# Attention scores on one core: the first k load as two transfers of 8 KB runs

## The chip, the cores and the metric

One core of one Trainium2 chip. The metric is the time of one execution on the device, in microseconds (us). In the profile, PE is TensorE's matmul, PEld its weight load, DVE is VectorE, ACT is ScalarE, POOL is GpSimd and SP is SyncE, which issues all 24 loads and outputs here (SPq in the page's table of DMA issues). "SPq" is SyncE's queue.

## The reference

```python
def setup_inputs():
    batch, heads, seq, dim = 8, 8, 512, 64
    # q and k: np.random.randn(batch, heads, seq, dim), float32

def reference(q, k):
    scale = 1.0 / np.sqrt(q.shape[-1])
    return (np.einsum('bhqd,bhkd->bhqk', q, k) * scale).astype(np.float32)
```

The inputs are 16.8 MB and the output is 67.1 MB, with little arithmetic between them.

## The kernel before

The batch is worked in four units of two. For each unit, one 2 MB transfer brings k and one brings q; GpSimd casts both to bf16 in two halves each (`s`); TensorE transposes them, VectorE and ScalarE copy the transposed tiles; matmuls make scores, and VectorE and ScalarE scale them into 4 MB output tiles. Loads and output tiles share one pool of three buffers (`big`), so the fourth unit's loads and the outputs wait until an earlier load has been cast: in the trace SyncE waits 4.9 us for GpSimd before it issues the fourth unit's k at 18.33 us, and the first evacuation, at 28.13, has waited 3.42 us for GpSimd.

```python
big_pool = ctx.enter_context(tc.tile_pool(name="big", bufs=3))
# ... (cut)
def load_and_cast(v):
    xf = big_pool.tile([P, 2, 2, J * D], f32, name="big")       # 128 x (k, q) x (s) x 2048
    both = []
    for x, src in enumerate((k_r, q_r)):
        nc.sync.dma_start(out=xf[:, x], in_=src[v].rearrange("p (s c) -> p s c", s=2))
    for x in range(2):
        xb = bf_pool.tile([P, JP, 2, D, 2], bf16, name="xb")
        wide = (1, RO)[x]
        for s in range(2):
            pinned(nc.gpsimd.tensor_copy(out=xb[:, :, s]..., in_=xf[:, x, s]...))   # (cut)
        both.append(...)
    return both
# ... (cut: transpose, rearrange)
def scores(v, t):
    o = big_pool.tile([P, 2, RO, S], f32, name="big")
    # ... 16 matmuls and 8 evacuations into o (cut)
    nc.sync.dma_start(out=out_r[v, t], in_=o.rearrange("p x i k -> p x (i k)"))
# ... (cut)
cast = [load_and_cast(v) for v in range(UNITS)]      # all loads are issued first
```

Of the kernel before, what the change touches and what calls it, by code (L numbers as in the profile page):

```python
# [1 line left out]

# [5 lines left out]


@with_exitstack  # L10
def kernel(
    ctx: ExitStack,
    tc: tile.TileContext,
    q: bass.AP,
    k: bass.AP,
    out: bass.AP,
):







    nc = tc.nc
    B, H, S, D = q.shape
    scale = 1.0 / (D ** 0.5)
    P = 128
    UNITS = B // 2
    N = H  # L30
    M = P // (2 * H)
    R = S // M
    J = R // 2
    RO = 8
    U = S // RO
    JP = J // 2
    JJ = J // RO // 2
    W = 8
    IW = W // JJ
    TILES = N // 2  # L40

    f32 = mybir.dt.float32
    bf16 = mybir.dt.bfloat16

    q_r = q.rearrange("(v b) g (m j) d -> v (b g m) (j d)", b=2, j=R)
    k_r = k.rearrange("(v b) g (m j) d -> v (b g m) (j d)", b=2, j=R)
    out_r = out.rearrange("(v b) (t x h) (u i) k -> v (b t) (h u) x (i k)", b=2, x=2, h=2, i=RO)

    consts = ctx.enter_context(tc.tile_pool(name="consts", bufs=1))

    big_pool = ctx.enter_context(tc.tile_pool(name="big", bufs=3))
    bf_pool = ctx.enter_context(tc.tile_pool(name="bf", bufs=6))
    t_pool = ctx.enter_context(tc.tile_pool(name="t", bufs=2))
    tpsum_pool = ctx.enter_context(tc.tile_pool(name="tpsum", bufs=2, space=bass.MemoryType.PSUM))
    psum_pool = ctx.enter_context(tc.tile_pool(name="psum", bufs=2, space=bass.MemoryType.PSUM))


    pinned = tc.keep_in_program_order

    n_evac = 0  # L60
    n_tp = 0

    def evacuate(dst, src):
        nonlocal n_evac
        if n_evac % 2 == 0:
            pinned(nc.scalar.mul(out=dst, in_=src, mul=scale))  # L66
        else:
            pinned(nc.vector.tensor_scalar(out=dst, in0=src, scalar1=scale, scalar2=None,  # L68
                                           op0=mybir.AluOpType.mult))
        n_evac += 1  # L70

    def half(h):
        return slice(h * D, (h + 1) * D)

    def words(ap):
        return ap.bitcast(f32)

    def load_and_cast(v):

        xf = big_pool.tile([P, 2, 2, J * D], f32, name="big")  # L80
        both = []
        for x, src in enumerate((k_r, q_r)):
            nc.sync.dma_start(out=xf[:, x], in_=src[v].rearrange("p (s c) -> p s c", s=2))
        for x in range(2):
            xb = bf_pool.tile([P, JP, 2, D, 2], bf16, name="xb")

            wide = (1, RO)[x]
            for s in range(2):
                pinned(nc.gpsimd.tensor_copy(  # L89
                    out=xb[:, :, s].rearrange("p (g i) d e -> p g e i d", i=wide),  # L90
                    in_=xf[:, x, s].rearrange("p (g e i d) -> p g e i d", e=2, i=wide, d=D)))
            both.append(words(xb.rearrange("p j s d e -> p j (s d e)")))
        return both

    def rearrange(tp, pattern, dst):

        nonlocal n_tp
        copy = (nc.vector.tensor_copy, nc.scalar.copy)[n_tp % 2]
        n_tp += 1
        for s in range(2):  # L100
            src = tp[half(s)].rearrange(pattern, n=N, h=2)
            for h in range(2):
                pinned(copy(out=dst(s, h), in_=src[:, h]))  # L103
                yield

    def transpose(v, kb, qb):


        kT = t_pool.tile([P, N, M, 2, J], bf16, name="kT")
        qz = qzs[v % 2]  # L110
        ts[v] = (kT, qz)
        kw = words(kT)
        qw = words(qz)
        for j0 in range(0, JP, W):
            tp = tpsum_pool.tile([P, W, P], f32, name="tp")
            for j in range(W):
                pinned(nc.tensor.transpose(out=tp[:, j, :], identity=identity, in_=kb[:, j0 + j]))  # L117
            yield
            yield from rearrange(tp, "d j (n h m) -> d h n m j",
                                 lambda s, h: kw[half(h), :, :, s, j0:j0 + W])  # L120
        for i0 in range(0, RO, IW):
            tp = tpsum_pool.tile([P, IW, JJ, P], f32, name="tp")
            for i in range(IW):
                for jj in range(JJ):
                    pinned(nc.tensor.transpose(out=tp[:, i, jj, :], identity=identity,  # L125
                                               in_=qb[:, RO * jj + i0 + i]))
            yield
            yield from rearrange(tp, "d i jj (n h m) -> d h i n m jj",
                                 lambda s, h: qw[half(h), i0:i0 + IW, :, h * U // 2:(h + 1) * U // 2]
                                 .rearrange("d i n (m s jj) -> d s i n m jj", s=2, jj=JJ)[:, s])  # L130

    def scores(v, t):

        kT, qz = ts[v]
        o = big_pool.tile([P, 2, RO, S], f32, name="big")
        for x in range(2):
            n = 2 * t + x
            for i in range(0, RO, 2):
                ps = psum_pool.tile([P, 2, S], f32, name="ps")
                for w in range(2):  # L140
                    pinned(nc.tensor.matmul(out=ps[:, w, :], lhsT=qz[:, i + w, n, :],  # L141
                                            rhs=kT[:, n].rearrange("d m s j -> d (m s j)"),
                                            start=True, stop=True))
                evacuate(o[:, x, i:i + 2, :], ps)
                yield
        nc.sync.dma_start(out=out_r[v, t], in_=o.rearrange("p x i k -> p x (i k)"))  # L146

    def take(steps, count):
        for _ in range(count):
            next(steps, None)  # L150

    identity = consts.tile([P, P], dtype=f32)
    make_identity(nc, identity)
    qzs = [consts.tile([P, RO, N, P], bf16, name=f"qz{n}") for n in range(2)]
    for qz in qzs:
        nc.vector.memset(qz, 0.0)  # L156
    cast = [load_and_cast(v) for v in range(UNITS)]

    ts = {}
    for _ in transpose(0, *cast[0]):  # L160
        pass
    for v in range(UNITS):
        ahead = transpose(v + 1, *cast[v + 1]) if v + 1 < UNITS else iter(())
        for t in range(TILES):
            for n, _ in enumerate(scores(v, t)):

                take(ahead, 1 if v == 0 else int(n in (0, 2, 3, 5, 6)))
        for _ in ahead:
            pass


# [1 line left out]
_INS = ['q', 'k']  # L173
_OUTS = [((8, 8, 512, 512), 'float32')]


# [23 lines left out]
```

## Time and profile before

| | before |
|---|---|
| median of 6 runs | 202.47 us (202.37 to 202.51) |
| span in the profile | 200.7 us |
| hardware DMA queue | 83.89 MB, 5504 packets, 98.3% of 16 engines' span |
| busiest engine | VectorE, 53% of the span |

Read it as a bandwidth-bound kernel: the DMA engines work nearly all of the span (98.3%) and no other engine does much over half of it (VectorE 53%).

### The profile page before, as it was taken

What the parts mean: (1) busy time and instruction counts of PE and PEld (TensorE: products, weight loads), DVE (VectorE), ACT (ScalarE), POOL (GpSimd) and SP (SyncE); (2) the same over time, 40 slices, a digit from 0 to 9 for tenths busy, and PEclk for the clock granted to TensorE, in tenths of its full rate; (3) what the DMA queues carried; (4) which work ended last, traced back from release to release, by engine and by line L of the source; (5) the groups of instructions that cost most, each with busy time, mean ns of one, the idle gap of its engine ahead of it and who ended that gap; (6) DMA issues with size and microseconds to landing.
All of it is one profiled execution on the core that took longest, in us unless ns stands there. A gap on an engine that the chain in (4) does not pass through costs nothing.

```text
span 200.7 us, 1143 instructions
## 1 busy us (share of the span) xinstructions
PE 105.3 (52%) x384; PEld 45.8 (23%) x384; DVE 106.8 (53%) x98; ACT 85.0 (42%) x97; POOL 39.5 (20%) x22
## 2 busy tenths in 40 slices
PE   0035758566657465478637496748585667510000
PEld 0034535223214131224313122312121111100000
DVE  6705538486475976485749357844444444630000
ACT  2004423864755629253844384366435243620000
POOL 1299999995000000000000000000000000000000
PEclk9999576999699999957999759975858858975555
DMA  6999999999999999999999999999999999999994
GB/s 206 424 444 437 421 421 441 434 395 421 434 424 441 428 431 431 433 426 434 431 428 424 434 441 424 431 431 434 424 431 434 431 424 431 428 437 428 428 428 199
DMA packets 5509, 83.95 MB, mean 418 GB/s; under 512 B 384, under 2 KB 384, under 8 KB 384
## 3 DMA queue, kind: packets, MB, share of 16 engines
q1 hardware_dynamic: 5504, 83.89, 98.3%
q8 instruction: 3, 0.05, 0.1%
q14 instruction: 2, 0.02, 0.0%
HBM read 16.78 MB, written 67.11 MB: 418 GB/s over the span
## 4 chain that ended last, share of the span: by engine, by line
DMA 40%; DVE 10%; PE 8%; ACT 6%; issue 1%; ACTq 0%; SPq 0%; DVEq 0%
DMA out_dram<-big 40%; DVE big L68 9%; PE ps L141 8%; ACT big L66 5%; ACT qz L103 1%; DVE qz L103 1%; ACTq L66 0%; SPq L146 0%; DVEq L68 0%
## 5 line engine op out<-in xcount | busy, mean ns | idle before, releaser
L141 PE MATMUL ps<-kT,qz 128*128 128x512 bf16 x256 | 87.6, 447 | 55.5 <-ACT big L66 41.6
L68 DVE TENSOR_SCALAR big<-ps 128x1024 f32<-128x1024 f32 x64 | 78.4, 1224 | 59.8 <-PE ps L141 37.2
L66 ACT ACTIVATE big<-ps 128x1024 f32<-128x1024 f32 x64 | 65.5, 1023 | 73.0 <-PE ps L141 37.2
L141 PEld LDWEIGHTS <-qz 128*128 128x128 bf16 x256 | 27.2, 106 | 111.0 <-issue 97.5
L89 POOL CAST xb<-big 128x2048 bf16<-128x2048 f32 x16 | 38.8, 2468 | 7.9 <-DMA big<-in_k_dram 7.3
L117 PE MATMUL tp<-identity,xb 128*128 128x128 f32 x64 | 11.6, 346 | 13.4 <-POOL xb L89 13.4
L103 ACT COPY kT<-tp 64x512 f32<-64x512 f32 x16 | 9.2, 577 | 15.3 <-PE tp L117 15.1
L103 DVE COPY kT<-tp 64x512 f32<-64x512 f32 x16 | 11.0, 686 | 6.3 <-PE tp L117 6.0
L117 PEld LDWEIGHTS tp<-identity,xb 128*128 128x128 f32 x64 | 10.5, 184 | 15.2 <-POOL xb L89 13.4
L103 DVE COPY qz<-tp 64x512 f32<-64x512 f32 x16 | 11.0, 687 | 2.7 <-PE tp L125 2.5
L103 ACT COPY qz<-tp 64x512 f32<-64x512 f32 x16 | 9.6, 602 | 2.9 <-PE tp L125 2.7
L125 PE MATMUL tp<-identity,xb 128*128 128x128 f32 x64 | 9.4, 300 | 2.5 <-ACT kT L103 2.5
L125 PEld LDWEIGHTS tp<-identity,xb 128*128 128x128 f32 x64 | 8.5, 156 | 4.3 <-issue 3.3
L156 DVE MEMSET qz<- 128x4096 uint32 x2 | 6.9, 3472 | 2.5 <-PEq L184 1.7
L103 ACT ACT_TABLE_LOAD x1 | 1.3, 1283 | 0.7 <-PEq L184 0.7
masks.py:199 POOL TENSOR_SCALAR_AFFINE_SELECT identity<-identity 128x128 f32<-128x128 f32 x1 | 0.3, 292 | 0.1
masks.py:197 POOL MEMSET identity<- 128x128 f32 x1 | 0.2, 204 | 0.3 <-POOLq L184 0.3
L184 POOL MEMSET const-float32-0.0<- 128x1 f32 x1 | 0.1, 98 | 0.2 <-issue 0.2
L184 POOL MEMSET const-bfloat16-1.0<- 128x1 bf16 x1 | 0.1, 101 | 0.0
L184 POOL MEMSET const-uint8-127<- 128x1 uint8 x1 | 0.1, 101 | 0.0
L184 POOL MEMSET const-float32-1.0<- 128x1 f32 x1 | 0.1, 98 | 0.0
## 6 DMA issues: line engine op xcount, KB each, us to landing
out_dram<-big SPq DMA_DIRECT2D x16, 4096.0 KB, 20.7
big<-in_k_dram SPq DMA_DIRECT2D x4, 2048.0 KB, 18.1
big<-in_q_dram SPq DMA_DIRECT2D x4, 2048.0 KB, 22.7
```

Of the source, the lines that this page charges most:

```text
L66: pinned(nc.scalar.mul(out=dst, in_=src, mul=scale))
L68: pinned(nc.vector.tensor_scalar(out=dst, in0=src, scalar1=scale, scalar2=None, op0=mybir.AluOpType.mult))
L89: pinned(nc.gpsimd.tensor_copy(out=xb[:, :, s].rearrange("p (g i) d e -> p g e i d", i=wide), in_=xf[:, x, s].rearrange("p (g e i d) -> p ...
L103: pinned(copy(out=dst(s, h), in_=src[:, h]))
L117: pinned(nc.tensor.transpose(out=tp[:, j, :], identity=identity, in_=kb[:, j0 + j]))
L125: pinned(nc.tensor.transpose(out=tp[:, i, jj, :], identity=identity, in_=qb[:, RO * jj + i0 + i]))
L141: pinned(nc.tensor.matmul(out=ps[:, w, :], lhsT=qz[:, i + w, n, :], rhs=kT[:, n].rearrange("d m s j -> d (m s j)"), start=True, stop=True))
L156: nc.vector.memset(qz, 0.0)
L184: nc = _bacc.Bacc("TRN2", target_bir_lowering=False, num_devices=1)
```

## The change

The intent: the first k load is 2 MB in runs of 16 KB, and GpSimd casts none of it until all has landed (at 8.53 us; the first cast starts at 8.58). Sent as two transfers, one for each half `s` of every row (8 KB runs), the first half is meant to be cast while the second is under way.

```diff
         for x, src in enumerate((k_r, q_r)):
-            nc.sync.dma_start(out=xf[:, x], in_=src[v].rearrange("p (s c) -> p s c", s=2))
+            halves = src[v].rearrange("p (s c) -> p s c", s=2)
+
+            for s in (slice(0, 1), slice(1, 2)) if v == x == 0 else (slice(0, 2),):
+                nc.sync.dma_start(out=xf[:, x, s], in_=halves[:, s])
```

## The prediction

> **What bounds the kernel now.** I read the page first: the table of busy times, the 40 slices, the DMA queues and the chain that ended last.
>
> ```profile
> span 200.7 us, 1143 instructions
> PE 105.3 (52%) x384; PEld 45.8 (23%) x384; DVE 106.8 (53%) x98; ACT 85.0 (42%) x97; POOL 39.5 (20%) x22
> ...
> DMA  6999999999999999999999999999999999999994
> GB/s 206 424 444 437 421 421 441 434 395 421 434 424 441 428 431 431 433 426 434 431 428 424 434 441 424 431 431 434 424 431 434 431 424 431 428 437 428 428 428 199
> ...
> q1 hardware_dynamic: 5504, 83.89, 98.3%
> ...
> DMA 40%; DVE 10%; PE 8%; ACT 6%; issue 1%; ACTq 0%; SPq 0%; DVEq 0%
> ```
>
> No engine is busy for more than 53% of the span, while the one hardware DMA queue fills 98.3% of the 16 DMA engines' span. The slices say where: only the first (206 GB/s) and the last (199) are half empty; the 38 between lie at 395 to 444 GB/s. The chain follows output transfers for 40% of the span and hops onto evacuations between them. That alone would look like a mixed bound, so I asked whether the DMA engines ever run out of queued work. The view of the DMA issues, cut so that each answer holds one issue, gives the time to landing; the timeline gives the start of the issue; the sum is the landing:
>
> - first k: 0.74 + 7.8 = 8.5 us. First q: 1.18 + 12.2 = 13.4. Second k: 1.66 + 16.6 = 18.3. Last q: 18.70 + 24.3 = 43.0.
> - first output: 36.81 + 17.1 = 53.9. Last output: 178.09 + 21.8 = 199.9.
>
> From the first k to the last q that is seven 2.10 MB loads in 34.5 us, 4.93 us each (425 GB/s); from the first output to the last it is fifteen 4.19 MB outputs in 146.0 us, 9.73 us each (431 GB/s). The first output is issued 6.2 us before the last load has landed, and the times to landing of the outputs (16.0 us at the least in those I read, 20.7 in the median) are all well over the 9.7 us that one output takes: when an output is issued, there are still some 6 us or more of older work in the queue. So the queue never runs dry, and computing can be late by about 6 us before the end notices.
>
> The start is the only place where the DMA engines wait for something:
>
> ```profile
> 0.74 0.39 SPq L83 DMA_DIRECT2D big<-in_k_dram  x1
> 1.18 0.42 SPq L83 DMA_DIRECT2D big<-in_q_dram  x1
> ...
> 8.58 34.34 POOL L89 CAST xb<-big 128x2048 bf16<-128x2048 f32 x14 [7.28 <-DMA big<-in_k_dram]
> ...
> 13.44 3.68 PE L117 MATMUL tp<-identity,xb 128*128 128x128 f32 x16 [13.44 <-POOL xb L89]
> ...
> 19.61 2.57 PE L125 MATMUL tp<-identity,xb 128*128 128x128 f32 x16 [2.49 <-ACT kT L103]
> ...
> 28.13 1.02 ACT L66 ACTIVATE big<-ps 128x1024 f32<-128x1024 f32 x1 [3.42 <-POOL xb L89]
> ...
> 36.81 20.11 SPq L146 DMA_DIRECT2D out_dram<-big  x3
> ```
>
> The reader is to see the relay of the opening: GpSimd waits 7.28 us for the whole first k, then casts fourteen tiles without a gap; the k transposes wait for two casts; the q transposes wait for ScalarE to empty the transposed k; the first evacuation waits for GpSimd to have done with the buffer that it will fill; the first output goes out at 36.81.
>
> [...] From the page of the profile, 98.3% of 16 x 200.7 us over the 5120 packets of data (5504 less 24 transfers x 16 small ones) is 617 ns for a 16 KB packet at the most[...].
>
> **The change part by part.** It touches one transfer of 24. The build shows one more DMA issue on the SyncE queue (two of 128 x 2048 elements for one of 128 x 4096) and a second DMA wait on GpSimd, before the second cast; the order on all engines stays.
>
> Removed: the first cast's wait for the second half of k. Half the transfer is half of 4.88 us (first k landing to first q landing), so the first half should land 2.45 us earlier, at about 6.1 us, and the first cast starts at 6.1 to 6.2 in place of 8.58.
>
> Added on SyncE: one issue, some 0.43 us. The other loads are issued that much later, q0 at about 1.6. They stand in a queue that is full until 8.5, so none of it shows.
>
> Added on the DMA engines: 128 data packets of 16 KB become 256 of 8 KB[...]
>
> Moved: the opening relay. GpSimd takes 34.34 / 14 = 2.45 us for a cast, 4.91 for the two of a load, and a load lands each 4.9 us: the two have the same pace, and GpSimd runs just one load behind. The first cast runs 6.1 to 8.6, the second half has then landed, the second runs 8.6 to 11.1. Then GpSimd needs q0, which lands at 13.4 to 13.5 as before. It waits 2.4 us there and stands where it stood. The head start is handed back at the third cast: 7.3 us of waiting becomes 4.8 + 2.4. From there on GpSimd does what it did, to 0.1 us.
>
> The k transposes do gain: 13.44 becomes about 11.1, and ScalarE ends its copies of k at about 17.2, not 19.5. The q transposes then wait for the q casts (13.5 + 4.9 = 18.4) in place of ScalarE, and start at 18.5, not 19.61: 1.1 us of the 2.4 is left. The first scores move from 23.57 to about 22.5. The first evacuation, however, waits for the eighth cast (8.58 + 8 x 2.45 = 28.2), which has not moved, so it stays at 28.1 to 28.2 and the 1.1 us end there. The first output may be issued some tenths earlier; it lies behind loads until 43.0 in any case.
>
> [...]
>
> **The rivals.**
> 1. *The head start reaches the end.* If the chain from the first cast set the end, 2.4 us would come off: 200.0 us, still within 2%. For it: the chain view names evacuations and matmuls in its early part, and GpSimd's first wait is real. Against it: the queue of loads is full until 43.0 and the outputs are queued 6 us ahead[...]. I give this 3%.
> 2. *The start-up itself changes.* First k lands at 8.5 although its bytes need 4.9: the windows view shows no packet until 1.5 us and 328 GB/s from 1.5 to 2.0, then 98 to 229 until 3.5; with half empty stretches like these the first slice is at 206 GB/s, and nearly 2 us of ramp are lost. If that ramp is paid per packet[...], 8 KB packets move half as much in it, and 0.3 to 0.9 us are lost for good: 202.8 to 203.4. If it is paid per engine once, nothing changes. [...] The profile doesn't decide between these; I take +0.3 or more to have a chance of 12%.
> 3. *The reads of 8 KB at a stride of 16 KB are slower in HBM.* Only 2.10 MB of 83.9 are read so. At half the rate that would be 4.9 us: 207 us, the only way that I see to over 2%. Nothing in the trace speaks for it; 1%.
> 4. *A new wait.* [...] an output is issued while at most two or three are in flight, so it should cost nothing.
>
> **Range and chances.** The runs of before lie within 0.1 us. Down to 202.2 for a quicker start-up or a tenth of drift, up to 202.9 for a part of rival 2 and some drift between chips. Within 2% means 198.4 to 206.5; only rival 3 leaves it upward, and I see nothing that leaves it downward, since the bytes alone need 83.89 MB / 431 GB/s = 194.6 us and the start-up, the turn from loads to outputs (10.9 us for the first output against 9.7) and the tail make up the rest: same 0.98, slower 0.01, faster 0.01.
>
> **What the changed profile would show.** Right: first cast at 6.1 to 6.2; a wait of about 2.4 us of GpSimd on q from some 11.1 to 13.5; k transposes at about 11.1; q transposes at 18.5, released by GpSimd and no longer by ScalarE; the first evacuation still at 28.1 to 28.3; 5504 + 144 = 5648 packets in the hardware queue, 400 of them small; the last load landing at 43.0 to 43.2, and a span of 200.6 to 201.0. Wrong: a last load that lands over 0.3 us later or earlier (rival 2 or 3), GpSimd without the wait at q0 (then q0 lands earlier than I think, and the first evacuation moves), or outputs that land closer to their issue than 10 us (then the queue does run dry, and the head start could matter).

The forecast's sum came to 202.5 us: 202.44 for the kernel before, 0 from the relay and less than 0.1 for the packets. That the outputs lie behind the loads in the queue is seen in the trace of before: its 24 transfers land in the order of their issue, the eight loads from 8.53 to 43.02 us and the sixteen outputs from 53.87 to 199.92.

## The result, and the profile after

The changed kernel takes 203.16 us (median of 6, 202.95 to 203.54) where the one before takes 202.47 us: ratio 1.0037, 95% interval 1.0024 to 1.0050. Ratios here and below are the mean time of one kernel's fast runs over that of the other's of the same rounds, so not quite the ratio of the medians quoted. That is within 2%, as forecast, but 0.7 us slower where less than 0.1 was forecast, and above the range's end of 202.9.

The lines of the page after that answer to those shown of before:

```profile
span 201.7 us, 1145 instructions
...
DMA  6999999999999999999999999999999999999993
GB/s 214 445 422 432 439 426 422 422 370 432 432 429 422 435 439 422 434 430 429 429 432 435 419 435 439 422 435 432 429 432 432 429 429 429 435 426 435 435 422 136
DMA packets 5653, 83.95 MB, mean 416 GB/s; under 512 B 400, under 2 KB 400, under 8 KB 400
...
q1 hardware_dynamic: 5648, 83.89, 98.0%
```

The counts are as foreseen: 144 packets more, 16 of them small. The first slice is no slower (214 against 206 GB/s). Two places differ: the ninth slice (370, before 395), and the last one (136, before 199).

The opening, from the timeline after (start, duration, instruction; in brackets the idle time before it and what ended it):

```profile
6.12 4.92 POOL L92 CAST xb<-big 128x2048 bf16<-128x2048 f32 x2 [4.82 <-DMA big<-in_k_dram]
...
11.10 3.67 PE L120 MATMUL tp<-identity,xb 128*128 128x128 f32 x16 [11.10 <-POOL xb L92]
...
13.49 29.43 POOL L92 CAST xb<-big 128x2048 bf16<-128x2048 f32 x12 [2.44 <-DMA big<-in_q_dram]
...
18.38 3.25 PE L128 MATMUL tp<-identity,xb 128*128 128x128 f32 x16 [3.60 <-POOL xb L92]
...
28.15 1.03 ACT L66 ACTIVATE big<-ps 128x1024 f32<-128x1024 f32 x1 [3.98 <-POOL xb L92]
...
43.92 4.86 POOL L92 CAST xb<-big 128x2048 bf16<-128x2048 f32 x2 [1.00 <-DMA big<-in_q_dram]
```

The first cast starts 2.46 us earlier, and GpSimd then waits 2.44 us for q: the head start is given back at the third cast. The first evacuation has not moved (28.15, before 28.13). So far all is as predicted. The last line is the one that is not: the last two casts wait 1.00 us for the last q. The line of before that answers to it:

```profile
43.17 4.86 POOL L89 CAST xb<-big 128x2048 bf16<-128x2048 f32 x2 [0.26 <-DMA big<-in_q_dram]
```

The last q lands 0.75 us later than before, though all loads ahead of it land on time. To see where, I asked for the stretch before that landing, 39.5 to 42.5 us, of both kernels (last three columns: granted clock, DMA share, GB/s by the start of packets). Before:

```profile
39.50:42.50 3.00, 2.28 (x15) 1.35 (x14) 1.53 (x2) 2.29 (x4) 3.00 (x2) 1.00 0.93 350
```

After:

```profile
39.50:42.50 3.00, 3.00 (x12) 2.08 (x11) 0.12 (x1) 1.70 (x3) 3.00 (x2) 0.50 0.96 300
```

Both fall well below the 429 GB/s of the stream around them (25 to 36 and 44 to 60 us, in both), the changed kernel further. This is the last load, with the first output standing behind it in the queue: the turn from loads to outputs. I call it the dip. The share of the engines stays near 1 (0.93 and 0.96) while the rate falls, so the engines are not idle; their packets take longer. The trace's packets show it: one of 16 KB that starts between 37 and 44 us takes 647 ns on average before and 690 after, where 614 is the average in the stream (25 to 36 us).

The landings, from the issue times and times to landing in the trace:

| us | before | after |
|---|---|---|
| first k whole | 8.53 | 8.54 |
| last k | 37.90 | 37.91 |
| last q | 43.02 | 43.77 |
| first output | 53.87 | 54.04 |
| last output | 199.92 | 200.82 |
| last k to last q | 5.13 | 5.86 |
| first to last output | 146.05 | 146.78 |

A load takes 4.9 us elsewhere (from the first k to the last, 4.88 to 4.91 each in before). So the dip costs 0.2 us before and almost 1.0 after at the last q; of the difference between the two kernels 0.17 us is left at the first output. The rest of the 0.9 us of this profiled run comes during the outputs: of the fifteen spacings between their landings eight are over 9.75 us, before four. This was the slowest run of six, and the split between the two places isn't the same in every run.

The trace keeps sixteen completions for each transfer (384 for the 24 of before), and the landing is the last of them. I read each as that of one of the sixteen engines, though the trace doesn't name it; their mean, called the average engine here, can then be followed as well:

| mean of the sixteen, us | last k | last q | first output | last output | last engine after the mean, last output |
|---|---|---|---|---|---|
| before | 37.45 | 42.60 | 52.44 | 198.68 | 1.23 |
| after | 37.31 | 42.92 | 52.75 | 198.93 | 1.89 |

For the average engine the last k comes 0.14 us sooner than before and the last q 0.32 later, and it stays 0.25 to 0.32 behind from there to the end: its outputs take no longer (146.2 us in both). So this part of the loss is made at the turn, and it is common to the sixteen: put in order, each completion of the last q comes 0.16 to 0.75 us later than its like of before. The rest, 0.66 us, is the lateness of the last completion alone, which falls further behind during the outputs: 1.28 us after the mean at the first output and 1.89 at the last, before 1.44 and 1.23 (the last but one ends 1.1 us after the mean in both). The average engine ends 2.2 us into the last slice of 5.04 us (136 GB/s), before 3.0 us into one of 5.02 (199).

### The profile page after: what moved, and what is told of

Read it like the earlier page. It is cut to its first block, busy times and chain, and to the rows that moved or that the text cites. A ratio compares the mean times of both kernels' runs of the same rounds, so it can differ in the third digit from the quotient of the medians.

```text
span 201.7 us, 1145 instructions
## 1 busy us (share of the span) xinstructions
PE 106.8 (53%) x384; PEld 46.4 (23%) x384; DVE 106.8 (53%) x98; ACT 85.1 (42%) x97; POOL 39.6 (20%) x22
## 3 DMA queue, kind: packets, MB, share of 16 engines
q1 hardware_dynamic: 5648, 83.89, 98.0%
## 4 chain that ended last, share of the span: by engine, by line
DMA 53%; PE 12%; ACT 9%; DVE 8%; POOL 5%; SPq 1%; issue 1%; ACTq 0%; DVEq 0%
DMA out_dram<-big 41%; DMA big<-in_k_dram 12%; PE ps L144 10%; DVE big L68 8%; ACT big L66 8%; POOL xb L92 5%; PE tp L128 2%; SPq L86 1%; ACT qz L106 1%; ACTq L66 0%; SPq L149 0%; DVEq L68 0%
## 5 line engine op out<-in xcount | busy, mean ns | idle before, releaser
L144 PE MATMUL ps<-kT,qz 128*128 128x512 bf16 x256 | 88.5, 450 | 57.0 <-ACT big L66 41.3
L120 PE MATMUL tp<-identity,xb 128*128 128x128 f32 x64 | 9.9, 311 | 11.1 <-POOL xb L92 11.1
L128 PE MATMUL tp<-identity,xb 128*128 128x128 f32 x64 | 11.6, 345 | 3.6 <-POOL xb L92 3.6
```

The source lines that it names most:

```text
L120: pinned(nc.tensor.transpose(out=tp[:, j, :], identity=identity, in_=kb[:, j0 + j]))
L128: pinned(nc.tensor.transpose(out=tp[:, i, jj, :], identity=identity, in_=qb[:, RO * jj + i0 + i]))
L144: pinned(nc.tensor.matmul(out=ps[:, w, :], lhsT=qz[:, i + w, n, :], rhs=kT[:, n].rearrange("d m s j -> d (m s j)"), start=True, stop=True))
```

## The experiments

Eighteen kernels ran; all gave correct results. In tables and text, the dip is measured by the time from the landing of the last k to that of the last q (4.9 us without a dip), and "outputs" as the time from the landing of the first output to that of the last. "Average engine" is the same time as "last k to last q", but between the means of the sixteen completions. Medians and ratios are of four to six runs; what is read from a trace is one profiled run of each kernel.

| run | first load | median us | ratio to before | last k to last q | average engine | outputs |
|---|---|---|---|---|---|---|
| before | 16 KB runs | 202.47 | | 5.13 | 5.15 | 146.05 |
| after | two of 8 KB runs | 203.16 | 1.0037 | 5.86 | 5.61 | 146.78 |
| e1 before again | 16 KB runs | 202.39 | 0.9995 | 5.08 | 5.12 | 146.09 |
| e2 after again | two of 8 KB runs | 203.02 | 1.0023 | 5.56 | 5.58 | 146.11 |
| e3 | two of 8 KB runs, second half first | 203.22 | 1.0034 | 5.46 | 5.49 | 146.52 |
| e4 | two of 64 partitions | 207.31 | 1.0235 | 4.90 | 4.90 | 146.38 |
| e5 | 16 KB runs, first q split | 202.70 | 1.0010 | 5.12 | 5.00 | 146.33 |
| e13 | 16 KB runs, second k split | 202.63 | 1.0009 | 5.00 | 4.92 | 146.25 |
| e6 | four of 4 KB runs | 202.99 | 1.0031 | 4.88 | 4.91 | 146.56 |
| e7 | one of 8 KB runs | 202.95 | 1.0025 | 5.52 | 5.20 | 145.77 |
| e8 | 16 KB runs, one small transfer more | 202.73 | 1.0011 | 5.18 | 5.05 | 146.20 |

The half width of the 95% intervals of the ratios is 0.0012 to 0.0014 in all of them.

### Is it real, and is it the relay? (e1 to e4)

My theory after the result: the transfers themselves (their packets or their number) put the DMA engines into a state that costs more at the turn. The rival: the relay, since casts and transposes run at other times than before and meet the stream differently. e1 and e2 are the two kernels unchanged but for a comment.

> The kernel before, unchanged but for a comment. All theories: 202.4 to 202.5 us and a ratio of 1.000 to within 0.001. Its trace is a second look at the turn from loads to outputs: if the 5.12 us from the landing of the last k to that of the last q in the trace of before is a property of the kernel, it is 5.0 to 5.3 again; if the turn is a matter of chance, it may be anything up to the 5.86 us that the changed kernel showed.

> The changed kernel, unchanged but for a comment. If its loss is real: 203.0 to 203.5 us, ratio 1.003 to 1.005, and a last q that lands 5.6 us or more after the last k. If the loss was chance of one compilation or chip: 202.4 to 202.6.

e1 repeats before to 0.1 us, dip included. e2 repeats the loss, 202.81 to 203.28 us, and a larger dip. The stretch of the dip in e1 and then in e2:

```profile
39.50:42.50 3.00, 2.28 (x15) 1.34 (x14) 1.54 (x2) 2.28 (x4) 3.00 (x2) 1.00 0.98 371
```

```profile
39.50:42.50 3.00, 2.28 (x13) 1.11 (x12) 1.81 (x2) 2.30 (x3) 3.00 (x2) 1.00 1.01 328
```

But its outputs take 146.11 us, as before: in this profiled run (202.81 us, the fastest of its five) the loss is that of the turn alone. So the loss has a part at the turn that came in both looks and a part in the outputs that comes and goes.

e3 keeps both transfers but swaps their order:

```diff
-            for s in (slice(0, 1), slice(1, 2)) if v == x == 0 else (slice(0, 2),):
+            for s in (slice(1, 2), slice(0, 1)) if v == x == 0 else (slice(0, 2),):
```

> The same two transfers of 8 KB runs, but the second half of k is sent first, so the first cast waits until both have landed (8.5 us) and the opening relay of GpSimd and TensorE is that of before. DMA theory (8 KB packets or one transfer more put the sixteen DMA engines out of step): slower as the changed kernel is, 203.0 to 203.5. Relay theory (transposes and casts that run earlier change what meets the turn from loads to outputs): as before, 202.4 to 202.6.

GpSimd's timeline of e3 is that of before, with the first cast at 8.47 and fourteen casts without a gap:

```profile
8.47 34.35 POOL L92 CAST xb<-big 128x2048 bf16<-128x2048 f32 x14 [7.17 <-DMA big<-in_k_dram]
43.40 4.85 POOL L92 CAST xb<-big 128x2048 bf16<-128x2048 f32 x2 [0.58 <-DMA big<-in_q_dram]
```

And it takes 203.22 us. The relay is that of before, the loss that of after: the relay theory falls.

e4 sends the first k as two transfers of 64 partitions with the 16 KB runs of before:

```diff
-            nc.sync.dma_start(out=xf[:, x], in_=src[v].rearrange("p (s c) -> p s c", s=2))
+            for p in (slice(0, P // 2), slice(P // 2, P)) if v == x == 0 else (slice(0, P),):
+                nc.sync.dma_start(out=xf[p, x], in_=src[v].rearrange("p (s c) -> p s c", s=2)[p])
```

> The first k in two transfers of 64 partitions each, with the 16 KB runs of before; each cast needs both, so the relay is that of before. If one transfer more[...] costs the time: 203.0 to 203.5. If the 8 KB packets or the early relay do: 202.4 to 202.6.

Neither expectation held, for a reason that I had not thought of. The windows view of e4 shows the first k at a flat half of the rate (210 GB/s where before has 426 between 5.0 and 7.5 us), with the engines' share near 1:

```profile
2.50:5.00 2.50, 0.00 (x0) 0.00 (x0) 2.50 (x1) 0.00 (x0) 0.00 (x0) 1.00 0.98 210
5.00:7.50 2.50, 0.00 (x0) 0.00 (x0) 1.70 (x2) 0.00 (x0) 0.00 (x0) 1.00 0.99 210
```

The whole first k lands at 13.11 us in place of 8.53, and those 4.6 us are nearly the whole loss of 4.8. That transfers of 64 partitions came at half the rate is measured; why, no run shows. So e4 doesn't say what a second transfer costs. It does show that there need be no dip at all (4.90).

### Which property of the split? (e5 to e8, e13)

> The first q split into two transfers of 8 KB runs in place of the first k: the same packets, bytes and count of transfers as the changed kernel, but in the steady stream, after the start-up. Start-up theory (8 KB packets in the ramp spread the sixteen DMA engines differently, and the spread costs at the turn from loads to outputs): as before, 202.4 to 202.6, last q 5.1 us after the last k. Count theory[...]: 203.0 to 203.3, last q 5.5 us or more after the last k.

```diff
+            for s in (slice(0, 1), slice(1, 2)) if v == 0 and x == 1 else (slice(0, 2),):
```

> The first k in four transfers of 4 KB runs. Start-up theory: a loss as in the changed kernel or larger, 203.0 to 204. Count theory: three transfers more in place of one, so up to three times the loss, 203.5 to 204.5. If the loss is a matter of how the work happens to fall on the engines, no order: 202.5 to 203.5.

```diff
+            if v == x == 0:      # dst and quarters: the rows of the first k in four parts of 1024
+                for s in range(2):
+                    for g in range(2):
+                        nc.sync.dma_start(out=dst[:, s:s + 1, g:g + 1], in_=quarters[:, s:s + 1, g:g + 1])
```

> The first k in one transfer, but with two runs of 8 KB for each partition, since its halves lie 64 bytes apart in the buffer. If the size of the packets in the start-up makes the loss: 203.0 to 203.3. If the count of transfers does: 202.4 to 202.6. The relay is that of before.

e7 sets the two halves of the first k 64 bytes apart in the buffer, so that one transfer has two 8 KB runs for each partition (two lines of a longer edit; every tile of `big` grows by the 64 bytes):

```diff
+        gap = 16 if v == 0 else 0
+        kf = raw[:, :2 * (J * D + gap)].rearrange("p (s c) -> p s c", s=2)[:, :, :J * D]
```

> The kernel before with one transfer more: 64 KB in runs of 512 B that nobody reads, right after the first k, which stays whole with its 16 KB runs. Its bytes cost 0.15 us at 431 GB/s (an estimate from the outputs' rate). Count theory: 203.0 to 203.5. Packet-size theory: 202.5 to 202.8.

```diff
+            if v == x == 0:
+                nc.sync.dma_start(out=extra, in_=src[v][:, :128])
```

> The second k split in two transfers of 8 KB runs, in place of the first. Same counts as the changed kernel. If the split costs only at the start of the stream: as the split of the first q, 202.5 to 202.8, last q 5.0 to 5.2 us after the last k. If any split costs: 203.0 to 203.3, last q 5.5 us or more after the last k.

```diff
-            for s in (slice(0, 1), slice(1, 2)) if v == x == 0 else (slice(0, 2),):
+            for s in (slice(0, 1), slice(1, 2)) if v == 1 and x == 0 else (slice(0, 2),):
```

The same split one or two loads later (e5, e13) costs 0.14 to 0.25 us with intervals that reach 1.000, and shows no larger dip. One transfer more (e8), whose bytes alone are worth 0.15 us (an estimate: 64 KB at the outputs' 431 GB/s), costs 0.28, also with an interval that reaches 1.000. Neither is the loss of the changed kernel. What loses 0.5 us or more is a first transfer with smaller runs, whether it is one transfer (e7), two (after, e2, e3) or four (e6). The medians alone don't part e2 from e5 (their intervals overlap); the dip of the average engine does: 5.5 to 5.6 us where the first k is split in two, 4.9 to 5.0 in e5 and e13. So the place matters: the start of the stream.

But the loss doesn't come by the same way in all of them. In e7 the first k lands at 8.96 us and in e6 at 9.14, 0.4 and 0.6 late, and their average engine has no clearly larger dip than before (5.20 and 4.91, before 5.15): their loss is at the start, where rival 2 of the prediction looked for it. That it is paid per packet is not shown: in after, with the same 256 packets of 8 KB as e7, the first k is whole at 8.54, in e2 and e3 at 8.26 and 8.42, no later than before, and it is the dip that is larger. In e7, too, the rest of the stream isn't that of before (a packet between 25 and 36 us takes 611 ns in place of 614), so its 202.95 us is not the first transfer alone.

### Is it the turn? (e9, e10, e15, e16)

If the dip comes from the first output standing behind the last load, an output that isn't there yet takes it away. A copy of 64 KB that reads the last q and that nobody uses is put on SyncE's queue ahead of the first output, so that SyncE waits for the last q (in e9 the copy is issued at 42.91 us and the first output at 43.52, where before issues it at 36.81); the order of transfers is pinned.

```diff
+        if v == t == 0:
+            pinned(nc.sync.dma_start(out=held, in_=last[0][:, 1, 1, :128]))    # last[0]: the last unit's load
-        nc.sync.dma_start(out=out_r[v, t], in_=o...)
+        pinned(nc.sync.dma_start(out=out_r[v, t], in_=o...))
```

> The kernel before, but the first output is held back on SyncE until the last q has landed (a 64 KB copy that reads the last q is queued ahead of it). Turn theory (the dip in the stream near 40 to 42 us comes from the first output standing in the queue behind the last load): the last q lands 4.9 us after the last k, not 5.1, and the end is later by the pause that the hold makes, some 1.5 to 2.5 us: 204 to 205. Other theory (the dip comes from something else, of the loads or the engines): still 5.1 us.

> The changed kernel with the same hold. Turn theory: its last q lands 4.9 us after the last k as well, not 5.6 to 5.9, and it runs as long as the held kernel before, to 0.2 us. Other theory: last q 5.5 us or more after the last k, and 0.4 us or more over the held kernel before.

The pins alone are not what these runs test: e11 and e12 below, started a little later, pin the same transfers without a hold, and the changed kernel is 0.68 us slower there.

e15 and e16 gate in the same way, but with a copy of 4 KB that reads the first cast of the last k (the copy is issued at 40.60 us in e15 and 40.54 in e16), for a shorter pause: `in_=cast[UNITS - 1][0][:16, 0, :D]`.

> The kernel before, with the first output issued only after the first cast of the last k (40.5 us). If the dip needs the output in the queue before about 40 us: last q 4.9 to 5.0 us after the last k, no pause or a short one, and 201.9 to 202.5. If the copy waits for both casts (42.9), it acts like the hold: 204 to 206.5.

> The changed kernel with the same gate at the first cast of the last k. Turn theory: its dip goes as well, last q 4.9 to 5.1 us after the last k, and it equals the gated kernel before to 0.2 us. If the changed kernel's loss has another part: 0.4 us or more over the gated kernel before.

| first output held until | before | after | after less before | last k to last q, before / after |
|---|---|---|---|---|
| not held | 202.47 | 203.16 | +0.69 | 5.13 / 5.86 |
| last q landed (e9, e10) | 206.46 | 206.35 | -0.11 | 4.88 / 4.89 |
| first cast of last k (e15, e16) | 204.34 | 204.19 | -0.15 | 4.90 / 4.94 |

In both held kernels GpSimd finds the last q there when it comes to it. Its timeline in e9 and then in e10:

```profile
8.67 39.25 POOL L90 CAST xb<-big 128x2048 bf16<-128x2048 f32 x16 [7.37 <-DMA big<-in_k_dram]
```

```profile
5.86 4.94 POOL L93 CAST xb<-big 128x2048 bf16<-128x2048 f32 x2 [4.56 <-DMA big<-in_k_dram]
13.24 34.33 POOL L93 CAST xb<-big 128x2048 bf16<-128x2048 f32 x14 [2.44 <-DMA big<-in_q_dram]
```

Sixteen casts without a gap in e9, and fourteen after the wait for the first q in e10: no wait of 0.26 or 1.00 us before the last two. The dip is gone in all four kernels, so it needs the first output in the queue behind the last load. That alone is not enough: e4 has the output there too (issued at 41.45 us, 4.6 us later than before, as its loads are), e6 holds none back, and neither has a dip (4.90 and 4.88). And the changed kernel, with the same two transfers of 8 KB runs, is now no slower than before (by medians 0.1 us faster): its loss passes through the overlap of the last load with the first output. The pause itself is dear, more than I expected for the hold (204 to 205) and for e15 (201.9 to 202.5, had the gate made no pause or a short one): the first output lands 13.9 us after the last q in e9, not 10.8, and the outputs take 147.0 us.

One caution: in these runs the outputs also come after a pause (20 GB/s in e9 and 25 in e10 from 41.5 to 44 us), so these four runs don't separate the dip from the slow outputs that follow it in some runs. For that the output has to come without a pause.

### Can the dip go without the pause? (e14, e17, e18)

The same gate, at the landing of the last k (37.9 us), while the last q still has some 4.9 us to go: a copy of 8 KB with `in_=last[0][:16, 0, 1, :128]`.

> The kernel before, with the first output issued only when the last k has landed (37.9 us, by a copy of a few KB queued ahead of it), so 1.5 us later than before and still 4 us before the stream of loads ends. If the output's mere presence in the queue during the last 2.5 us makes the dip: as before, last q 5.1 us after the last k, 202.4 to 202.7.

> The changed kernel with its first output issued only when the last k has landed. Turn theory: last q 4.9 to 5.1 us after the last k, and the loss of 0.6 us is gone: 202.2 to 202.6. If the loss has its source elsewhere and the dip is only a companion: 202.9 to 203.3.

> The gated kernel before once more, for the same chip and rounds: 202.3 to 202.6, last q 4.9 to 5.1 us after the last k. Turn theory: equal to the gated changed kernel to 0.2 us.

| gate at the last k | median us | ratio to before | last k to last q | average engine | outputs | last output, mean | last engine after it |
|---|---|---|---|---|---|---|---|
| e14 before | 202.51 | 0.9999 | 4.99 | 4.91 | 146.24 | 198.73 | 1.08 |
| e18 before again | 202.66 | 1.0013 | 5.22 | 4.97 | 146.03 | 198.61 | 1.19 |
| e17 after | 202.86 | 1.0018 | 5.04 | 4.91 | 146.93 | 198.67 | 1.47 |

In e17 the stretch of the dip is at full rate, although the output, issued at 38.45, stands in the queue for 4.3 us before the last q lands:

```profile
39.50:42.50 3.00, 2.28 (x14) 1.24 (x13) 1.70 (x2) 2.30 (x3) 3.00 (x2) 1.00 1.04 434
```

There is no pause either (the first output lands 10.42 us after the last q), and the changed kernel takes 0.2 us more than the gated kernel before on the same chip, where the ungated pair differed by 0.5 to 0.7. Neither expectation of e17 held, 202.2 to 202.6 or 202.9 to 203.3; that of e18, equal to 0.2 us, just held (its own time and dip, 5.22, fell a little outside theirs), and the intervals of the two ratios (half widths 0.0013 and 0.0014) don't tell e17 from e18. By the landings, e17 keeps slow outputs, 146.9 us in place of 146.0 (ten of the fifteen spacings are over 9.75 us, in e18 two). The average engine shows what that is: it ends at 198.67 us in e17, between e14 and e18, so it has nothing left of the loss of after; the last completion is still 0.3 to 0.4 us further behind than in e14 and e18. So the part that the average engine loses at the turn goes with the gate, and the late last completion is another part, which comes and goes (1.30 us after the mean in e2, 1.66 in e3, 1.17 in e1) and whose cause no run shows. For the kernel before, the gate changes nothing that the runs can tell: 202.51 and 202.66 against 202.47. No version beat the kernel before.

### Does it depend on when the stream comes? (e11, e12)

In the first eight runs the dip was smaller where the loads came later, so both kernels were started later: SyncE waits for a GpSimd memset of elements that the first load overwrites.

```diff
+        if v == 0:
+            nc.gpsimd.memset(xf[:, 0, :, :1], 0.0)
```

> The kernel before with its first load issued some 0.7 us later (SyncE waits for a GpSimd memset of a few elements that the load overwrites). In the runs so far the dip at the turn was smaller where the stream of loads came later. If that is a rule, the last q lands 4.9 to 5.0 us after the last k and the delay costs less than itself: 202.6 to 202.9. If not, 203.1 to 203.3, the delay in full.

> The changed kernel with the same later start. If the dip shrinks with lateness: the last q lands under 5.3 us after the last k, and the end is 203.0 to 203.3, no later than without the delay. If not: 203.7 to 203.9.

e11 took 202.73 us (last k to last q 5.28 us), e12 203.41 (5.51), where the kernel before took 202.62 in the same rounds. The delay of 0.4 us (first k at 8.89) cost only 0.1 us in e11, but the dip is not smaller, and the changed kernel is again 0.7 us slower. Lateness is no rule.

## Why the prediction was wrong

Point by point:

- *What bounds the kernel*: right. The stream of transfers sets the end; nothing that computing did changed it (e3: the relay of before, and 203.22 us).
- *The relay*: right in nearly each number. First cast 6.12 (predicted 6.1 to 6.2), wait for q 2.44 (2.4), k transposes 11.10 (11.1), q transposes 18.38, released by GpSimd (18.5), first evacuation 28.15 (28.1 to 28.3). Two small misses: the first scores start at 22.81 (22.5), and the first output is issued at 37.03, 0.2 us later than before and not some tenths earlier. Its worth for the end was put at 0, and e3, which takes the relay away and keeps the loss, agrees.
- *SyncE's added issue*: right, nothing of it shows; the last k lands at 37.91, before at 37.90.
- *Packets*: the count was right (5648, 400 small), and so was the mark that would show the step wrong, "a last load that lands over 0.3 us later": it landed at 43.77, 0.75 later.
- *The step that failed* is the sum, 0 from the relay and less than 0.1 from the packets. For the stream it held only a fixed cost for each packet; no run shows that cost. It lacked a term for the turn: "the turn from loads to outputs (10.9 us for the first output against 9.7)" was seen, and carried over as a constant. It isn't one. The dip there needs the first output behind the last load, and its size differs with how the stream was begun; it grew from 5.13 to 5.86 us (5.08 and 5.56 in the second looks), for the average engine by 0.46 us in both, and taking the output away took the loss away (e9 against e10). The working also followed the stream as one; that the last of the sixteen completions may come further behind the others (1.89 us after their mean, before 1.23) had no term either.
- *Rival 2* named the right event (8 KB packets at the start) and a size of 0.3 to 0.9 us that holds the measured 0.7, but at the wrong place: it foresaw a first k that lands late. That is what e7 and e6 show (0.4 and 0.6 us late), not the changed kernel; that its size holds the measured loss is luck. There a sooner start came, for which the range had left room down to 202.2: for the average engine the first k is whole at 7.84 to 7.95 us in the six undelayed kernels with this split (after, e2, e3, e10, e16, e17), and at 8.08 to 8.20 in those with a first k in one transfer of 16 KB runs. The turn takes back more than that. The rival got too little weight, 12% for 0.3 us or more, so that the range ended at 202.9.
- *Rivals 1, 3 and 4*: none came. The bytes at a stride of 16 KB came at full rate (first k whole at 8.54, before at 8.53), and one small transfer more (e8) cost 0.28 us, of which its bytes explain 0.15.

What stays open: why two transfers of 8 KB runs at the start, and not the same two one load later, make the dip larger 29 us later, and why in some runs the last completion then falls behind during the outputs. How far the sixteen are apart before the turn doesn't explain it: the completions of the last k are spread over 0.97 us in before and 0.96 in after, and e6, with as wide a spread (1.07), has no dip. The trace doesn't name the engine of a packet, so I could not follow one engine through.

## What to carry to other kernels

Where the queue of transfers never runs dry, an earlier start of the first consumer was handed back at the next landing (a first cast 2.46 us earlier, then a wait of 2.44): look for the second wait before counting on the end of the first. And a saturated queue wasn't indifferent to how it was fed: here, runs of another size at its start cost 0.5 to 0.75 us (after, e2, e3, e6, e7) with the DMA engines' queue filling 98.0% of their span (the page of after), part of it where an output stood behind the last load, so a forecast of zero for a touched transfer deserves a range of some tenths and a look at where the stream changes direction. A landing in this trace is the last of sixteen completions, here up to 1.89 us after their mean; before calling a transfer slow, look at the mean of the sixteen too.
